# An encoder layer on one core: the second 512 tokens' rows into the opening's buffers, longer leads, gate tiles three ahead, and residual rows as whole tiles

## The chip, the cores and the metric

The kernel runs on one core of a Trainium2 chip. The core has five engines with instruction streams of their own: TensorE (PE, matmuls and transposes by matmul), VectorE (DVE), ScalarE (ACT), GpSimd (POOL) and SyncE (SP), which issues nearly all transfers in this kernel; sixteen DMA engines carry them out. The metric is device time in microseconds; smaller is better.

## The reference

Two sequences, one of 1024 tokens (the prompt, s = 0) and one of 2048 (the sample, s = 1), with 1024 channels, go through one layer of a bidirectional encoder. Sixteen learned meta tokens stand in front of each.

```python
xn = _rmsnorm(h, g_pre)
proj = xn @ w_in + b_in                                  # 6672 columns
na_q, na_k, na_v, na_z, ml_qk, ml_v, ml_z, ml_o, ml_g, mg = jnp.split(proj, SPLIT_IDX, axis=-1)
ya = _neighbourhood_attention(na_q, na_k, na_v, na_rpb)  # 8 heads of 64, windows of 8 x 16 on a grid 64 wide
ya = (ya * jax.nn.silu(na_z)) @ w_a
yb = (_mlstm_branch(ml_qk, ml_v, ml_g, ml_o, ml_conv_w, ml_head_g) * jax.nn.silu(ml_z)) @ w_b   # 4 heads of 128, both directions
ga, gb = jnp.split(jax.nn.sigmoid(mg), 2, axis=-1)
y = (ga * ya + gb * yb) @ w_out
return h + _rmsnorm(y, g_post)
```

All is float32.

## The kernel before

**Matmuls.** A float32 product is made of three matmuls on split operands (`mm3`, lines 155 to 157): high by high, high by low, low by high. Every weight and every activation is therefore split into a rounded high part (ACT) and a remainder (DVE). Weights come in units of 512 KB: `wload` loads a raw unit into a `wraw` tile, `wpump` (L250, L251) splits it into `whi` and `wlo`, and both parts are also stored, so that later uses load the parts (L243) and no raw unit. Before the opening ends raw units lie in a pool of its own (`xp`, four buffers); after it in the main pool `wp` (two buffers).

**Two streams of work.** `dense` is a generator for the projections and the output: it goes through `PLAN`, a list of column groups (m: mLSTM columns, n: attention columns, g: gate columns) for stretches of 1024 tokens, and then six output blocks of 512 tokens ("f", two of the prompt and four of the sample). `sparse` is a generator for the mixers in the order mLSTM of the prompt, attention of the prompt, mLSTM of the sample, attention of the sample. `run` (L1617) weaves them: each step of `sparse` yields a number of microseconds, and `dense` is advanced until its own yields have used that number up. The numbers are constants at L118: `A_NA` for a step of attention, `A_A` for a step of the mLSTM outputs, `A_D` for a step of the mLSTM states, `A_G` for one of its gates; a dense step of 512 columns counts 0.235 for each matmul and one of 256 columns 0.12. Each attention unit (a head and a quarter of the columns of eight grid rows) takes four steps: scores, scaling, transposition, output. The order of PE's instructions is the order in which these generators write them. The order on the other engines and on SP's queue is made by a planner, which simulates the program and takes what is ready, in the order of writing where several are. Each engine then runs in that order, and an instruction that waits holds up those behind it.

**Opening.** The first 512 tokens' activations come transposed (`xt`, four loads) and in rows (`tokens`, four loads of 512 KB into tiles `xr`). `xsplit` scales and splits the transposed ones. The rows serve the RMS norm: `rsum` squares and sums them on ACT (tile `xsq`, L287) and takes the inverse root by Newton steps on DVE (L141 to L146), `rdiag` (L299, L301) writes it into diagonals, and `rrows` (L307) lets PE broadcast it. The projections of these tokens are evacuated with that factor, so they wait for the broadcast in their third or fourth column; its place in PE's order is fixed in `group`. Nine buffers named `xr` in `xp` hold the opening's tiles of both kinds and the meta tokens. The second 512 tokens' transposed tiles are loaded in the opening into four `xr` buffers of `wp`; their rows are loaded later, in `build_half` (L394), into these same four buffers, one behind each `xsplit`. The pool `xp` is closed at the end of the opening.

**Attention.** `na` (L733) prepares the first head in six steps of `na_prep`: loads first, then splits. Between the loads and the first split lie `14 - 8 * s` steps of `A_NA`, that is 14 for the prompt and 6 for the sample.

**mLSTM states.** `ml_states` (L1089) runs once for each of four heads. It loads two blocks, yields `A_D`, begins the convolution (`cv`), yields, ends it (`kf`, L1112), yields, and then transposes `kf` on PE (L1148) in a loop. For the first head the loads go into memory that the gates' tiles free.

**Output blocks.** `final` (L1429) makes a block of 512 tokens. For each of eight column tiles `ft` it multiplies the two branches by their weights (branch 1, then 0), and DVE multiplies each product by a gate tile `tg` (L1465) loaded from DRAM. `gates(ft + 2)` is called at the end of step `ft`. Gate tiles of both branches share four buffers under the tag `stT`. The sum is split (`mh` L1468, `mlo` L1469) and multiplied by `w_out` (L1495 to L1497). Beside that second half runs `yload` for the next block, whose `yr` tiles have four buffers under the tag `st`. The norm and the residual of a block are a generator, `final_out` (L1545), advanced twice in each `ft` of the next block: it loads half rows of the input (128 x 512, `xres`, three ahead) into `st` buffers too, and DVE adds them (L1568). The last block has a list of its own, `self.last`, whose tiles lie in `st` and `wraw` buffers.

Of the kernel before, what the change touches and what calls it, by code (L numbers as in the profile page):

```python
# [9 lines left out]
F32 = mybir.dt.float32  # L10
# [3 lines left out]
ALU = mybir.AluOpType  # L14
# [3 lines left out]
P = 128  # L18
TCARGS = dict(schedule_with_timeline_sim=True)
D = 1024  # L20
# [15 lines left out]
WU = 264  # L36
# [78 lines left out]

NBW = 4
C512, C256 = 0.235, 0.12
A_NA, A_D, A_A, A_G = 1.12, 1.63, 1.84, 1.3  # L118


class K:
# [218 lines left out]
    def opening(self, xp):  # L340

        nc, wp, cp = self.nc, self.wp, self.cp
# [11 lines left out]
        toks = self.tokens(0, 0, (0, 1), xp, 9)  # L354
# [3 lines left out]
        self.xnext = [self.xtload(0, 512, e, wp, 4) for e in (0, 1)]  # L358
        self.wload(4)
        self.xnext += [self.xtload(0, 512, e, wp, 4) for e in (2, 3)]  # L360
        x = self.xparts()
        self.xs.append(tuple(x))
        g = self.gpre.rearrange("p (k a) -> p k a", a=1).to_broadcast([P, KT, NM])
# [16 lines left out]
        dg, dm = self.rdiag(res[0], dt), dt[:NM, 512:]  # L380
# [13 lines left out]
    def build_half(self, s, t0, res):  # L394

        nc, wp = self.nc, self.wp
        if (s, t0) in self.xkept:
            yield
            yield "scaled"
            x = []  # L400
# [7 lines left out]
        if s == 0:  # L408
# [7 lines left out]
            if not self.done:  # L416
# [1 line left out]
                nc.tensor.matmul(p[:, :KT], self.ident, g, start=True, stop=True)  # L418
                g = self.cp.tile([P, KT], F32, name="gx")
                nc.vector.tensor_copy(g, p[:, :KT])  # L420
            x, toks, r = self.xparts(), [], []
            for e in range(4):
                self.xsplit(x, xts[e], e, 0, g)
                if not self.done:
                    toks += self.tokens(s, t0, (e,), wp, 4)
                    self.wflush(2)
                yield
            res.append(tuple(x))
            if self.done:
                return  # L430
            self.wflush()
            yield
            yield from self.rsum(toks, r)
            nc.vector.tensor_copy(self.rc[:, 4:8], r[0])
            dg = self.rdiag(r[0], toks[0][0])
            self.rwait[s, t0] = lambda: self.rrows(dg, self.rr[:, 1], "sm")
        else:
            toks, r = self.tokens(s, t0, range(4), wp, 4), []
            yield
# [14 lines left out]
            x = self.xparts()  # L454
# [278 lines left out]
    def na(self, s, rts):  # L733
# [3 lines left out]
        with tc.tile_pool(name=f"na{s}{rts[0]}", bufs=1, side="right", reuse_waits="tile") as np_:  # L737
# [10 lines left out]
            prep = self.na_prep(np_, s, rows, heads, 0)  # L748
            for k in range(6):
                next(prep, None)  # L750
                for _ in range(2 if k else 14 - 8 * s):
                    yield A_NA
            self.na_bias(rows, heads, 0)
            cur, nxt = self.head, None
# [334 lines left out]
    def ml_states(self, mp, s, h, g, NB, sts):  # L1089
# [42 lines left out]

        load(0)
        load(1)
        yield A_D
        conv_a(0)
        yield A_D
        conv_b(0)
# [290 lines left out]
    def final(self, s, b, nxt):  # L1429
# [10 lines left out]
        def gates(ft):  # L1440
            if ft < KT:
                tgs[ft] = []
                for br in (1, 0):
                    tg = fp.tile([P, n], F32, name="tg", tag="stT", bufs=4)
                    nc.sync.dma_start(tg, self.GT[s][8 * br + ft][:, t0:t0 + n])
                    tgs[ft].insert(0, tg)

        gates(0)
        gates(1)
        for ft in range(KT):  # L1450
            w = self.wtake(1)[0]
            ms = tgs.pop(ft)
            for br in (1, 0):
                for k in range(4 * br, 4 * br + 4):
                    while k not in self.yk:
                        if next(self.ygen) == "wait":
                            yield True
                p = self.psum("pj", [P, 512])
                for k in range(4 * br, 4 * br + 4):
                    self.mm3(p, w[0][:, k, :], w[1][:, k, :], yh[:, k], yl[:, k], start=k % 4 == 0, stop=k % 4 == 3)  # L1460
                    if k % 4 == 1:
                        yield 6 * C512
                if not br:
                    self.wdone()
                nc.vector.scalar_tensor_tensor(ms[br], ms[br], 1.0, p, op0=ALU.add, op1=ALU.mult)  # L1465
                if not br:
                    nc.vector.tensor_tensor(ms[0], ms[0], ms[1], op=ALU.add)
                    nc.scalar.activation(mh[:, ft], ms[0], AF.Copy)  # L1468
# [76 lines left out]
    def final_out(self, s, t0, yt, ssq, a, b):  # L1545

        nc, fp, i = self.nc, self.wp, self.i
        src, out = (i["x_prompt"], self.o[0]) if s == 0 else (i["x_sample"], self.o[1])
        todo = [(tt, slice(t0 + tt * P, t0 + tt * P + P), c) for tt in range(a, b) for c in (slice(0, 512), slice(512, D))]
        xr = [self.last.pop(0) for _ in todo] if self.last else []  # L1550
# [12 lines left out]
        nc.vector.tensor_scalar(sv[:, a:b], sv[:, a:b], 1.0 / D, 16.0 * EPS, op0=ALU.mult, op1=ALU.add)  # L1563
        r = self.rsqrt8(fp, sv[:, a:b], [P, b - a])
        yield
        for j, (tt, rows, c) in enumerate(todo):
            y = yt[tt][:, c]
            nc.vector.scalar_tensor_tensor(y, y, r[:, tt - a:tt - a + 1], xr[j], op0=ALU.mult, op1=ALU.add)  # L1568
            nc.sync.dma_start(out[rows, c], y)
            load(j + 3)  # L1570
            yield


    def dense(self, ctx):
# [4 lines left out]
        with tc.tile_pool(name="xp", bufs=1, side="right", reuse_waits="tile") as xp:  # L1579
            self.wrp = xp, 4  # L1580
            self.opening(xp)
        self.y = self.fout = None
        meta, post = True, None
        for j, (s, t0, cols) in enumerate(PLAN):
# [108 lines left out]
```

## Time and profile before

| what | value |
|---|---|
| median of 3 runs | 2869.04 us (2866.74 to 2869.99) |
| the profiled execution | 2862.5 us |
| its span, first to last instruction | 2860.7 us |
| mean granted TensorE clock in it | 0.993 |
| PE busy | 2798.8 us |
| DVE busy | 1799.6 us |
| ACT busy | 1307.1 us |
| moved by DMA | 661.43 MB, mean 231 GB/s |

How to read the lines that follow. A row of waits names the engine and line that waited, what released it, the sum of the waits, their number and the longest. A row of a stretch gives its bounds, its length, the busy time of PE, PE's weight loads, DVE, ACT and POOL, each with the number of instructions, then the granted clock (1.00 is full), the share in which the DMA engines were busy, and GB/s. A row of the timeline gives the start, the length, the engine, the line, the operation, its output and inputs, and in brackets how long the engine had stood idle and what released it. A row of the chain of work gives the start, the length and the step; that chain is followed backwards from the last instruction.

### The profile page before, as it was taken

The numbers are of one execution on the slowest core, as the hardware profiler recorded it, in microseconds if no ns is written. First come the engines' busy times: TensorE is split into PE (matmuls) and PEld (weight loads), VectorE is DVE, ScalarE is ACT, GpSimd is POOL, SyncE is SP. The second block draws the span as 40 slices with busy tenths as digits, with TensorE's granted clock in tenths as the row PEclk, the third lists the DMA queues.
The fourth block names the chain that finished last, engine by engine and source line by source line (L and its number), as shares of the span: only waits on it lengthen the run. The fifth ranks groups of instructions, "written<-read, shape, count | busy, mean of one in ns | idle before, by whom it ended". The sixth has DMA issues, their size and how long they took to land.

```text
span 2860.7 us, 49242 instructions
## 1 busy us (share of the span) xinstructions
PE 2798.8 (98%) x17312; PEld 2489.1 (87%) x17312; DVE 1799.6 (63%) x4931; ACT 1307.1 (46%) x3135; POOL 16.1 (1%) x103
## 2 busy tenths in 40 slices
PE   8999999999999999999999999999999999999998
PEld 7998898999799988888988888888887988889887
DVE  4232688576466654556667666574678787787844
ACT  5112556444444443355455555453455554545421
POOL 0000000000000000000000000000000000000000
PEclk9999999999999999999999999999999999999999
DMA  9455768755876654675656786656679898998875
GB/s 370 162 187 194 236 211 296 275 182 177 312 236 188 179 166 133 187 278 164 206 194 207 245 283 188 192 185 192 202 243 337 278 326 271 293 291 252 291 261 179
DMA packets 385001, 661.43 MB, mean 231 GB/s; under 512 B 51984, under 2 KB 200928, under 8 KB 384752
## 3 DMA queue, kind: packets, MB, share of 16 engines
q1 hardware_dynamic: 383632, 655.58, 69.5%
q0 software_dynamic: 1120, 2.69, 0.4%
q8 instruction: 137, 2.24, 0.3%
q14 instruction: 112, 0.92, 0.1%
HBM read 455.90 MB, written 202.22 MB: 230 GB/s over the span
## 4 chain that ended last, share of the span: by engine, by line
PE 81%; DMA 10%; DVE 5%; ACT 1%; issue 1%; SPq 1%; DVEq 0%; ACTq 0%
PE pj L155 14%; PE pj L156 13%; PE pj L157 13%; PE pj L575 6%; PE pj L576 6%; PE pj L577 6%; PE pj L1497 3%; PE pj L1495 3%; PE pj L1496 3%; PE sm L884 3%; PE tr L872 2%; DMA tg<-gt 2%; PE sm L157 1%; PE sm L156 1%; PE sc L848 1%
## 5 line engine op out<-in xcount | busy, mean ns | idle before, releaser
L155 PE MATMUL pj<-xh,whi 128*128 128x512 f32 (+1 forms) x1792 | 706.2, 394 | 2.4 <-ACT whi L250 1.8
L156 PE MATMUL pj<-xl,whi 128*128 128x512 f32 (+1 forms) x1792 | 690.4, 385 | 0.1
L157 PE MATMUL pj<-xh,wlo 128*128 128x512 f32 (+1 forms) x1792 | 688.8, 384 | 0.3 <-DVE wlo L251 0.3
L575 PE MATMUL pj<-whi,xh 128*128 128x256 f32 (+3 forms) x1576 | 451.0, 286 | 0.0
L576 PE MATMUL pj<-wlo,xh 128*128 128x256 f32 (+3 forms) x1576 | 444.6, 282 | 0.0
L577 PE MATMUL pj<-whi,xl 128*128 128x256 f32 (+3 forms) x1576 | 444.4, 282 | 0.0
L157 PEld LDWEIGHTS pj<-xh,wlo 128*128 128x128 f32 x1792 | 337.9, 189 | 72.1 <-DVE wlo L251 0.5
L155 PEld LDWEIGHTS pj<-xh,whi 128*128 128x128 f32 x1792 | 338.3, 189 | 62.2 <-ACT whi L250 2.6
L156 PEld LDWEIGHTS pj<-xl,whi 128*128 128x128 f32 x1792 | 338.5, 189 | 56.8 <-issue 1.0
L575 PEld LDWEIGHTS pj<-whi,xh 128*128 128x128 f32 (+1 forms) x1576 | 294.4, 187 | 1.6 <-ACT st L505 0.3
L576 PEld LDWEIGHTS pj<-wlo,xh 128*128 128x128 f32 (+1 forms) x1576 | 294.1, 187 | 1.0
L577 PEld LDWEIGHTS pj<-whi,xl 128*128 128x128 f32 (+1 forms) x1576 | 294.0, 187 | 0.9
L1495 PE MATMUL pj<-whi,mh 128*128 128x256 f32 x768 | 220.7, 287 | 5.1 <-ACT mh L1468 2.6
L855 ACT ACTIVATE prb<-sc,mx 128x384 f32<-128x384 f32 (+2 forms) x192 | 120.0, 625 | 223.2 <-DVE mx L851 216.9
L1497 PE MATMUL pj<-whi,mlo 128*128 128x256 f32 x768 | 217.5, 283 | 2.3 <-DVE mlo L1469 2.3
L1496 PE MATMUL pj<-wlo,mh 128*128 128x256 f32 x768 | 217.2, 283 | 0.0
L875 DVE TENSOR_TENSOR pts<-tr,pts 96x512 fp32r<-96x512 f32 (+2 forms) x192 | 131.5, 685 | 84.3 <-ACT pts L874 83.0
L155 PE MATMUL pj<-yh,whi 128*128 128x512 f32 x384 | 156.6, 408 | 5.9 <-DVE tg L1465 5.9
L874 ACT ACTIVATE pts<-tr 96x512 fp32r<-96x512 f32 (+2 forms) x192 | 114.0, 594 | 103.2 <-PE tr L872 102.5
L1495 PEld LDWEIGHTS pj<-whi,mh 128*128 128x128 f32 x768 | 146.2, 190 | 7.5 <-ACT mh L1468 3.1
L156 PE MATMUL pj<-yl,whi 128*128 128x512 f32 x384 | 152.0, 396 | 0.0
L157 PE MATMUL pj<-yh,wlo 128*128 128x512 f32 x384 | 152.0, 396 | 0.0
(271 smaller groups left out, 5043.8 us busy)
## 6 DMA issues: line engine op xcount, KB each, us to landing
whi<-wh SPq DMA_DIRECT2D x176, 512.0 KB
wlo<-wl SPq DMA_DIRECT2D x176, 512.0 KB
wraw<-wu SPq DMA_DIRECT2D x64, 512.0 KB
wh<-whi SPq DMA_DIRECT2D x64, 512.0 KB
wl<-wlo SPq DMA_DIRECT2D x64, 512.0 KB
gt<-st SPq DMA_DIRECT2D x96, 256.0 KB
tg<-gt SPq DMA_DIRECT2D x96, 256.0 KB
xt<-xt SPq DMA_DIRECT2D x32, 512.0 KB
```

Of the source, the lines that this page charges most:

```text
L155: mm(out, ah, bh, start=start, stop=False)
L156: mm(out, ah, bl, start=False, stop=False)
L157: mm(out, al, bh, start=False, stop=stop)
L575: nc.tensor.matmul(o, xh, wh, start=k == 0, stop=False)
L576: nc.tensor.matmul(o, xh, wl, start=False, stop=False)
L577: nc.tensor.matmul(o, xl, wh, start=False, stop=k == KT - 1)
L855: nc.scalar.activation(pr_[:, :N].rearrange("p (b a c) -> p b a c", b=4, c=8), sc[:, :N].rearrange("p (a b c) -> p b a c", b=4, c=8), AF.E ...
L874: nc.scalar.activation(pts[:ks, :, 0, :], pt[:ks], AF.Copy)
L875: nc.vector.tensor_tensor(pts[:ks, :, 1, :], pt[:ks], pts[:ks, :, 0, :].bitcast(F32), op=ALU.subtract)
L1495: nc.tensor.matmul(o, mh[:, k, xs], wh, start=k == 0, stop=False)
L1496: nc.tensor.matmul(o, mh[:, k, xs], wl, start=False, stop=False)
L1497: nc.tensor.matmul(o, ml[:, k, xs], wh, start=False, stop=k == KT - 1)
```

## The change

Seven edits are made.

1. The rows of the second 512 tokens are loaded at the end of the opening's loads, as four more tiles `xr` in `xp`, where nine buffers now serve thirteen tiles; `build_half` loads none and no longer writes out all remaining weight parts in a step of its own. `xp` stays open until the broadcast of these tokens has been written.
2. The step costs `A_NA` and `A_A` go from 1.12 to 1.1 and from 1.84 to 1.82.
3. The lead of the first attention head goes from 14 to 17 steps for the prompt and stays at 6 for the sample.
4. The first head of each mLSTM yields 6.0 us more between its loads and its convolution.
5. Gate tiles are asked for three steps ahead instead of two. Those of branch 1 stay under the tag `stT`, those of branch 0 go under `st`, with four buffers each.
6. `final_out` loads whole rows (128 x 1024) into the two `wraw` buffers of `wp`, two ahead, and asks for the next one after the second half of a tile has been used.
7. The last block still takes its residual tiles from `self.last`.

```diff
-A_NA, A_D, A_A, A_G = 1.12, 1.63, 1.84, 1.3
+A_NA, A_D, A_A, A_G = 1.1, 1.63, 1.82, 1.3
...
         self.xnext += [self.xtload(0, 512, e, wp, 4) for e in (2, 3)]
+        self.toks = self.tokens(0, 512, range(4), xp, 9)
         x = self.xparts()
...
-            x, toks, r = self.xparts(), [], []
+            x, r = self.xparts(), []
             for e in range(4):
                 self.xsplit(x, xts[e], e, 0, g)
                 if not self.done:
-                    toks += self.tokens(s, t0, (e,), wp, 4)
                     self.wflush(2)
                 yield
             res.append(tuple(x))
             if self.done:
                 return
-            self.wflush()
-            yield
-            yield from self.rsum(toks, r)
+            yield from self.rsum(self.toks, r)
             nc.vector.tensor_copy(self.rc[:, 4:8], r[0])
-            dg = self.rdiag(r[0], toks[0][0])
-            self.rwait[s, t0] = lambda: self.rrows(dg, self.rr[:, 1], "sm")
+            dg = self.rdiag(r[0], self.toks[0][0])
+
+            def rows():
+                self.rrows(dg, self.rr[:, 1], "sm")
+                self.xp.close()
+            self.rwait[s, t0] = rows
...
-                for _ in range(2 if k else 14 - 8 * s):
+                for _ in range(2 if k else 17 - 11 * s):
                     yield A_NA
...
         load(1)
-        yield A_D
+        yield A_D + (0.0 if h else 6.0)
         conv_a(0)
...
-                    tg = fp.tile([P, n], F32, name="tg", tag="stT", bufs=4)
+                    tg = fp.tile([P, n], F32, name="tg", tag=("st", "stT")[br], bufs=4)
...
-        gates(0)
-        gates(1)
+        for ft in range(3):
+            gates(ft)
...
-                    gates(ft + 2)
+                    gates(ft + 3)
...
-        def load(j):
-            if len(xr) <= j < len(todo):
-                x = fp.tile([P, 512], F32, name="xres", tag="st", bufs=4)
-                nc.sync.dma_start(x, src[todo[j][1], todo[j][2]])
-                xr.append(x)
-
-        for j in range(3):
-            load(j)
+        def load(tt):
+            if tt < b:
+                xr.append(fp.tile([P, 4 * WU], F32, name="xres", tag="wraw", bufs=2)[:, :D])
+                nc.sync.dma_start(xr[-1], src[t0 + tt * P:t0 + tt * P + P, :])
+
+        if not self.last:
+            load(a)
+            load(a + 1)
         yield
...
-        for j, (tt, rows, c) in enumerate(todo):
-            y = yt[tt][:, c]
-            nc.vector.scalar_tensor_tensor(y, y, r[:, tt - a:tt - a + 1], xr[j], op0=ALU.mult, op1=ALU.add)
-            nc.sync.dma_start(out[rows, c], y)
-            load(j + 3)
-            yield
+        for tt in range(a, b):
+            x = None if self.last else xr.popleft()
+            for c in (slice(0, 512), slice(512, D)):
+                y = yt[tt][:, c]
+                nc.vector.scalar_tensor_tensor(y, y, r[:, tt - a:tt - a + 1], self.last.pop(0) if self.last else x[:, c], op0=ALU.mult, op1=ALU.add)
+                nc.sync.dma_start(out[t0 + tt * P:t0 + tt * P + P, c], y)
+                if c.start:
+                    load(tt + 2)
+                yield
```

More of the change, by code (lines that the diff above doesn't have):

```diff
@@ L1548, in final_out @@
         src, out = (i["x_prompt"], self.o[0]) if s == 0 else (i["x_sample"], self.o[1])
-        todo = [(tt, slice(t0 + tt * P, t0 + tt * P + P), c) for tt in range(a, b) for c in (slice(0, 512), slice(512, D))]
-        xr = [self.last.pop(0) for _ in todo] if self.last else []
-        def load(j):
-            if len(xr) <= j < len(todo):
-                x = fp.tile([P, 512], F32, name="xres", tag="st", bufs=4)
-                nc.sync.dma_start(x, src[todo[j][1], todo[j][2]])
-                xr.append(x)
-        for j in range(3):
-            load(j)
+        xr = deque()
+        def load(tt):
[5 more added lines that the diff above has]
+            load(a + 1)
         yield
@@ L1578, in dense @@
         self.requests()
-        with tc.tile_pool(name="xp", bufs=1, side="right", reuse_waits="tile") as xp:
-            self.wrp = xp, 4
-            self.opening(xp)
+        self.xp = ExitStack()
+        xp = self.xp.enter_context(tc.tile_pool(name="xp", bufs=1, side="right", reuse_waits="tile"))
+        self.wrp = xp, 4
+        self.opening(xp)
         self.y = self.fout = None
```

## The prediction

> **What bounds the kernel now.** I read the page first, then the busy time by stages, then who made TensorE wait, then the granted clock right behind each wait, and last the chain of work around the places that the diff touches.
>
> ```profile
> span 2860.7 us, 49242 instructions
> ...
> PE 2798.8 (98%) x17312; PEld 2489.1 (87%) x17312; DVE 1799.6 (63%) x4931; ACT 1307.1 (46%) x3135; POOL 16.1 (1%) x103
> ...
> PE 81%; DMA 10%; DVE 5%; ACT 1%; issue 1%; SPq 1%; DVEq 0%; ACTq 0%
> ```
>
> TensorE (PE) is the bound: it idles 2860.7 - 2798.8 = 61.9 us. The change removes and adds no matmul, so it can win no more than this and what a lowered clock costs. Where the 61.9 us lie (the first number of a row's body is its length, the second PE's busy time):
>
> ```profile
> 0.00:100.00 100.00, 91.67 (x591) 81.16 (x592) 41.61 (x101) 43.20 (x74) 1.20 (x18) 0.97 0.86 320
> ...
> 300.00:350.00 50.00, 47.70 (x308) 43.56 (x307) 31.19 (x84) 26.78 (x70) 2.56 (x14) 0.97 0.68 218
> ...
> 750.00:800.00 50.00, 46.28 (x208) 37.22 (x207) 25.03 (x48) 20.67 (x37) 0.00 (x0) 0.97 0.97 348
> 800.00:1150.00 350.00, 350.00 (x2337) 322.09 (x2336) 204.69 (x524) 151.11 (x335) 1.74 (x16) 1.00 0.57 174
> 1150.00:1200.00 50.00, 43.54 (x349) 42.36 (x348) 21.83 (x81) 16.29 (x48) 0.00 (x0) 0.93 0.61 172
> ...
> 2100.00:2740.00 640.00, 614.20 (x3902) 551.06 (x3902) 514.42 (x1201) 325.70 (x769) 2.04 (x4) 0.99 0.89 288
> 2740.00:2861.00 121.00, 108.06 (x721) 98.53 (x719) 54.36 (x142) 16.93 (x56) 0.00 (x0) 0.99 0.64 231
> ```
>
> So 8.3 us in the opening, 2.3 where the first mLSTM starts, 3.7 where the first attention starts, 6.5 where the second mLSTM starts, 25.8 while the output blocks run beside the second attention, 12.9 in the last block and the tail. Who held PE:
>
> ```profile
> PE tr L872 <- DVE prb L864: 12.9, 9, 3.7
> PE pj L155 <- DVE tg L1465: 5.9, 5, 2.3
> PE tr L1148 <- DVE kf L1112: 5.4, 1, 5.4
> PE sm L307 <- ACT xr L299: 4.5, 1, 4.5
> ...
> PE sc L847 <- DVE stk L825: 3.2, 1, 3.2
> PE pj L1495 <- ACT mh L1468: 2.6, 1, 2.6
> ```
>
> Three waits occur once each (L1148, L307, L847 behind stk), and the diff has an edit for each of the three. The first two rows, 12.9 and 5.9 us, belong to the output blocks. A wait is also paid a second time. Right after each longer one the granted clock (the third number from the end) is halved:
>
> ```profile
> 60.30:65.30 5.00, 5.00 (x11) 3.30 (x12) 2.29 (x4) 2.19 (x4) 0.00 (x0) 0.50 1.02 410
> 314.50:317.80 3.30, 3.30 (x17) 3.30 (x17) 1.80 (x7) 1.50 (x7) 0.33 (x2) 0.50 1.06 395
> 771.90:775.20 3.30, 3.30 (x10) 2.52 (x9) 2.34 (x6) 1.78 (x4) 0.00 (x0) 0.50 1.05 404
> 1191.60:1195.00 3.40, 3.40 (x17) 3.40 (x18) 2.16 (x5) 2.42 (x7) 0.00 (x0) 0.50 0.60 168
> 2174.80:2178.00 3.20, 3.20 (x11) 2.61 (x10) 2.86 (x7) 1.65 (x2) 0.00 (x0) 0.50 1.02 308
> 2211.00:2215.60 4.60, 4.60 (x24) 4.60 (x23) 3.19 (x7) 3.02 (x8) 0.00 (x0) 0.50 0.70 255
> ...
> 2662.90:2666.20 3.30, 3.30 (x12) 2.72 (x11) 3.27 (x7) 0.67 (x2) 0.00 (x0) 0.50 1.05 404
> ```
>
> PE is busy throughout these stretches at half speed, so each costs half its length: 2.5, 1.65, 1.65, 1.7, 1.6, 2.3 and 1.65 us.
>
> **Opening: rows of the second 512 tokens.** Before, their four loads are issued inside build_half, after each xsplit; the squares, the Newton steps and the diagonal follow, and PE's row broadcast (L307) waits for them.
>
> ```profile
> 46.37 0.59 SPq L330 DMA_DIRECT2D xr<-x_prompt  x1
> ```
>
> ```profile
> 51.33 1.09 ACT L250 ACTIVATE whi<-wraw 128x1056 fp32r<-128x1056 f32 x1 [4.48 <-DMA mq<-st]
> 52.32 1.04 ACT L287 ACTIVATE xsq<-xr 128x1024 bf16<-128x1024 f32 x1
> ```
>
> The last of the four is issued at 46.37, the first square starts at 52.32, and ACT had stood idle 4.48 us in front of it. After the change the loads go into buffers whose readers are the first xsplits and squares, so by my estimate they are issued some 20 us sooner. Four squares (4 x 1.04 us) then fit into ACT's idle time ahead of 51.33, and the chain behind them is done 5 us or more sooner, against a wait of 4.5. What covers it: PE has matmuls of the second half until the broadcast. Gain 4.5 + 2.5 = 7.0 us. Low end 4.5, if a smaller wait still halves the clock. High end of cost: the 2 MB enter a DMA system that is 0.86 busy in this stage, at 320 GB/s 6.6 us of transfer, and whatever is queued behind them on SP moves by up to that: stores of weight parts and, before, these same rows. The next raw weights are not needed before the second job, so I charge nothing, and 2 us in the range. Keeping the opening's pool open until the broadcast delays only loads that go into its memory later, the first mLSTM's constants, which that stage (300 to 350) does not need so early.
>
> **First attention: 14 steps of lead become 17.** The lead is 17 x 1.10 - 14 x 1.12 = 3.0 us of dense work more before PE's first score.
>
> ```profile
> 771.48 0.44 PE L848 MATMUL sc<-kx,qB 128*128 128x384 f32 x1 [0.47 <-DVE kx L829]
> ```
>
> ```profile
> 756.39 9.48 DMA xt<-xt
> ```
>
> The wait is 3.2 + 0.47 = 3.7 us: the head's splits stand behind the next half's, which wait for an xt load of 9.48 us. 3.0 of it goes and 0.7 stays. Whether the clock still drops with that is open; I take half of 1.65. Gain 3.0 + 0.8 = 3.8, ends 1.5 and 5.4. Late next is kx, the 0.47.
>
> **mLSTM: 6 us more before the first convolution, in both.** In the second one the load is issued at 1179.25, when the gates' buffers come free, and lands 5.93 us later; on DVE kf then stands behind a decay tile whose load ends at 1190.67.
>
> ```profile
> 1179.25 5.93 DMA raw<-mk
> ...
> 1187.04 3.63 DMA um<-ud
> ```
>
> PE comes 6.0 us later to a wait of 5.4: it goes, with 0.6 to spare. Gain 5.4 + 1.7 = 7.1; low end 3, because the decay load may move along. In the first mLSTM the 2.3 us come later, in its second step, where ACT is crowded; the lead moves PE and ACT alike. I take nothing (ends -4.0 and +1.5).
>
> The Trainium skill (TensorE: Matmul & The Clock Gate, What's actually happening) says that the clock falls back to half after an idle window of about 3.4 us. By that rule the 0.7 us left at the attention's start cost no clock, and its term would be 3.0 + 1.65 = 4.65. The trace sides with it only in part: waits of 2.3 us in all (300 to 350) were followed by a halved clock.
>
> **Step costs 1.12 to 1.10 and 1.84 to 1.82.** From the loops: attention takes 264 + 520 steps, the mLSTM outputs 136 + 232. 784 x 0.02 + 368 x 0.02 = 23.0 us less dense work is laid beside the sparse work, 12.0 + 3.3 more in the leads. About 8 us of matmuls move behind the last attention unit. That is PE work at the same price, so 0. The side effect is density: a unit has 4 x 0.02 = 0.08 us less cover. From 800 to 1150, most of it beside the first attention, PE is busy 350.00 of 350 us at 1.12, so I price it at 0 there; it speaks only beside the output blocks.
>
> **Output blocks: gates three ahead, residual rows elsewhere.** DVE works in order; while it waits for a load there, the scaling of attention (prb) stands behind it.
>
> ```profile
> DVE tg L1465 <- DMA tg<-gt: 26.4, 15, 4.3
> ...
> DVE yo L1568 <- DMA xres<-x_sample: 8.5, 4, 3.3
> DVE yo L1568 <- DMA xres<-x_prompt: 3.2, 3, 1.9
> ```
>
> ```profile
> 2174.44 0.83 PE L872 MATMUL tr<-ident,prb 128*128 128x128 f32 x4 [2.07 <-DVE prb L864]
> 2302.26 0.63 PE L872 MATMUL tr<-ident,prb 128*128 128x128 f32 x4 [1.77 <-DVE prb L864]
> 2418.23 0.63 PE L872 MATMUL tr<-ident,prb 128*128 128x128 f32 x4 [1.95 <-DVE prb L864]
> 2662.68 0.94 PE L872 MATMUL tr<-ident,prb 128*104 128x128 f32 x4 [1.96 <-DVE prb L864]
> ```
>
> ```profile
> 2279.27 6.08 DMA xres<-x_prompt
> ...
> 2418.28 8.10 DMA tg<-gt
> ...
> 2646.82 6.58 DMA xres<-x_sample
> ```
>
> One ft step is 24 matmuls, 5.6 us at the code's own 0.235, plus the attention's share; a third step of lead exceeds the longest gate wait of 4.3. Gates no longer share four buffers between both branches, and residual rows no longer compete with the yr loads for st. The transfers grow from 256 to 512 KB, in half the number, with the lead of three half rows kept. Best case: all 5.9 us of tg, these four prb waits (7.75), and the clock behind two of them (1.6 + 1.65) go: 16.9 us. Worst: nothing, because DMA is 0.89 busy over this stage and an earlier load makes another one later. I take half, 8.5. The other waits (heads' loads, L1495 behind mh, the last weights) I leave as they are; they will fall in other places, which I hold for +-6 us. The last block's residual tiles now wait for the last gates, with half a block of time.
>
> **Sum.** 7.0 + 3.8 + 7.1 + 8.5 = 26.4 us; less 1.4 for small new waits in the crowded stages: 25. The profiled execution took 2862.5 us (span 2860.7), 6.5 below the median 2869.0 of the runs shown. Its like after the change is 2837.5, and the median forecast 2869 - 25 = 2844. About 0.2%, 5.7 us, is what a measurement of this kernel can tell from no change.
>
> **Rivals.** First: the output blocks are bound by transfers, and earlier loads gain nothing there. For it: share 0.89 at 288 GB/s over 640 us. Against: the last 121 us are at 0.64 and still have a gate wait, and the opening moved 410 GB/s. Then 17.9 us remain: 2851. Chance 0.20. The Trainium skill (DMA: Bandwidth & Descriptors, Specifications) gives about 358 GB/s of HBM per core, a limit by which such stretches are full; the 410 GB/s here pass it.
>
> Second: the leads only move the wait, to kx and to the decay tile, and the output blocks gain nothing either. Opening 7.0, attention 1.5, mLSTM 3: gain 11.5, 2857.5. For it: 0.47 behind kx and the um row. Chance 0.10.
>
> Third, slower: the third gate pair (512 KB) and larger residual tiles (1 MB against 768 KB at a block's start) put 0.75 MB in front of the heads' loads in SP's one queue, 2.6 us at 288 GB/s. ACT and DVE then stand at a head's split more often. Its price from the trace: the mh wait of 2.6 us, followed by 2.3 of halved clock, 4.9. Twenty-four heads, about five per block, run in this stage. At one more such wait in each of five blocks it is 24.5 us: 2869 - 17.9 + 24.5 = 2875.6. It decides from four (19.6 against 17.9). For it: DVE is 514.4 of 640 busy. Against: these loads do land somewhere today, in the same blocks. Chance 0.08.
>
> Fourth: the edit in the opening does nothing, because SP still issues the rows late or ACT orders the squares late: 19.4 without its 7.0 and with small waits counted, 18 us, 2851. Chance 0.05.
>
> **Chances and range.** The forecast has 0.57, with its own range 2834 to 2854. From 2829 (16.9 in the output blocks and 4.0 in the first mLSTM) to 2863 all but the slower case and a poor second rival are held. Faster by over 0.2%: 0.57 + 0.20 + 0.05 + 0.05 (half of the second, with its spread) = 0.87, which I lower to 0.85; the same 0.06; slower 0.09.
>
> **What would show it.** Right: no wait at L307 and L1148, at most 1 us at L847 behind stk or kx; no 0.50 clock after them; the xsq squares of the second rows before 50 us; DVE's waits for tg under 10 us. Wrong: PE's busy time unchanged but its idle time in the output blocks above 35 us; ACT or DVE waiting longer for kr, qr or whi; new waits of PE in the first 50 us for weights.

## The result and the profile after

| | before | after |
|---|---|---|
| median of 7 runs | 2867.28 us (2864.1 to 2870.18) | 2849.97 us (2837.03 to 2858.18) |
| the profiled execution | 2862.5 us | 2845.39 us |
| its span | 2860.7 us | 2843.6 us |

The ratio of the times is 0.9933, with an interval of 0.9913 to 0.9954, which is 19 us less. On another occasion, beside the kernel before on the same chip, the changed kernel gave 0.9906 (0.9889 to 0.9923), 27 us less. Both profiled executions lie 4.6 to 4.8 us below their medians, so their spans can be compared as they stand. The head of the page of the changed kernel:

```profile
span 2843.6 us, 49257 instructions
...
PE 2795.7 (98%) x17312; PEld 2488.8 (88%) x17312; DVE 1796.3 (63%) x4931; ACT 1306.4 (46%) x3135; POOL 16.1 (1%) x103
```

PE's idle time fell from 61.9 to 2843.6 - 2795.7 = 47.9 us, which is 14.0; its busy time fell by 3.1 with the same matmuls. Together 17.1, the difference of the spans. Each trace is of one execution: the seven of the changed kernel spread over 21 us, and a second trace of it (the last run below) idles 23.8 us in the output blocks where this one idles 20.7, so differences of a few microseconds between the stages of two traces are not told from this spread. The stages of the changed kernel, in the columns of the prediction's table of stretches:

```profile
0.00:100.00 100.00, 96.16 (x641) 85.58 (x642) 42.64 (x103) 43.46 (x75) 1.20 (x18) 1.00 0.87 325
300.00:350.00 50.00, 49.53 (x329) 45.25 (x328) 32.78 (x84) 26.21 (x68) 2.62 (x14) 1.00 0.70 248
750.00:800.00 50.00, 46.34 (x229) 39.58 (x228) 22.75 (x46) 18.93 (x36) 0.00 (x0) 0.93 0.99 325
1150.00:1200.00 50.00, 47.10 (x378) 45.11 (x377) 25.03 (x91) 18.45 (x56) 0.00 (x0) 1.00 0.52 156
1200.00:2100.00 900.00, 894.76 (x4682) 756.65 (x4680) 560.88 (x1743) 459.26 (x1165) 4.08 (x22) 1.00 0.65 209
2100.00:2740.00 640.00, 619.31 (x3989) 559.44 (x3988) 515.45 (x1202) 325.06 (x777) 2.04 (x4) 0.99 0.90 292
2740.00:2861.00 121.00, 93.12 (x597) 84.25 (x596) 49.59 (x131) 13.16 (x44) 0.00 (x0) 0.97 0.56 200
```

The fifth stage of the kernel before, which the prediction did not show:

```profile
1200.00:2100.00 900.00, 897.70 (x4741) 761.24 (x4740) 563.44 (x1745) 458.81 (x1167) 4.08 (x22) 1.00 0.64 209
```

Idle time of PE by stage, before and after (the last stage ends at 2843.6): opening 8.3 to 3.8, first mLSTM 2.3 to 0.5, first attention 3.7 to 3.7, start of the second mLSTM 6.5 to 2.9, its continuation 2.3 to 5.2, output blocks 25.8 to 20.7, last block and tail 12.6 to 10.5 (the prediction's 12.9 counts up to 2861; the span ends at 2860.7). Who held PE in the changed kernel (line numbers below the edits are two or three higher):

```profile
PE tr L874 <- DVE prb L866: 12.3, 7, 3.3
PE sc L849 <- ACT prb L857: 5.9, 4, 3.0
PE pj L577 <- DMA whi<-wh: 2.9, 1, 2.9
PE sc L155 <- ACT qh L1228: 2.6, 1, 2.6
...
PE tr L1150 <- DVE kf L1114: 1.2, 1, 1.2
```

The broadcast's wait (4.5), the gates' (5.9) and the wait behind stk (3.2) have no row left, and kf went from 5.4 to 1.2. New are the weight loads and qh. The transposition behind prb still costs what it did, 12.3 against 12.9, and the score behind ACT's prb costs 5.9 against 4.5. Three places in the changed kernel's timeline, first on PE, then on SP and ACT in the opening, then on ACT at 1877:

```profile
790.67 0.49 PE L577 MATMUL pj<-whi,xh 128*128 128x264 f32 x1 [2.88 <-DMA whi<-wh]
791.94 0.59 PE L578 MATMUL pj<-wlo,xh 128*128 128x264 f32 x1 [0.79 <-DMA wlo<-wl]
1882.54 0.33 PE L155 MATMUL sc<-qh,kh 128*128 128x128 f32 x1 [2.63 <-ACT qh L1228]
```

```profile
20.33 2.86 SPq L330 DMA_DIRECT2D xr<-x_prompt  x4
```

```profile
30.28 1.07 ACT L287 ACTIVATE xsq<-xr 128x1024 bf16<-128x1024 f32 x1
...
40.51 1.04 ACT L287 ACTIVATE xsq<-xr 128x1024 bf16<-128x1024 f32 x1
```

```profile
1877.18 5.00 ACT L321 ACTIVATE xh<-xt,gpre 128x512 fp32r<-128x512 f32 x8
```

In the opening the last row load was issued at 46.37 before; now the four leave from 20.33 on and the squares fall between 30 and 42 us. At 1877 eight splits of a next half, 5.00 us on ACT, stand in front of the split qh that the second mLSTM needs; that is where the shifted streams meet. Behind both places on PE, the weights and qh, the clock is halved, in these stretches:

```profile
790.90:795.00 4.10, 3.31 (x15) 3.06 (x15) 0.24 (x1) 0.00 (x0) 0.00 (x0) 0.50 1.05 307
1885.00:1889.50 4.50, 4.50 (x17) 3.92 (x17) 3.52 (x13) 2.49 (x7) 0.00 (x0) 0.50 1.01 366
```

Last, the output blocks from DVE's and ACT's side, from 2100 us on, before and then after:

```profile
ACT yh L1403 <- DMA yr<-ya: 17.4, 12, 4.8
ACT yh L1403 <- DMA yr<-yb: 1.4, 1, 1.4
...
DVE yl L1404 <- ACT yh L1403: 10.7, 8, 5.0
```

```profile
DVE yl L1406 <- ACT yh L1405: 20.8, 14, 3.7
...
ACT yh L1405 <- DMA yr<-yb: 21.9, 11, 3.9
ACT yh L1405 <- DMA yr<-ya: 13.4, 10, 2.6
```

DVE's 26.4 us of waits for gates have no row any more. ACT's waits for the branches' rows (yr), which now share the buffers `st` with the gates of branch 0, rose from 18.8 to 35.3 us, and DVE's for yh behind them from 10.7 to 20.8.

### The profile page after: what moved, and what is told of

It reads as the page before. It is cut to its first block, busy times and chain, and to the rows that moved or that the text cites. A ratio compares the mean times of both kernels' runs of the same rounds, so it can differ in the third digit from the quotient of the medians.

```text
span 2843.6 us, 49257 instructions
## 1 busy us (share of the span) xinstructions
PE 2795.7 (98%) x17312; PEld 2488.8 (88%) x17312; DVE 1796.3 (63%) x4931; ACT 1306.4 (46%) x3135; POOL 16.1 (1%) x103
## 4 chain that ended last, share of the span: by engine, by line
PE 85%; DMA 8%; DVE 5%; ACT 1%; issue 1%; SPq 0%; DVEq 0%; ACTq 0%
PE pj L155 15%; PE pj L156 14%; PE pj L157 14%; PE pj L577 6%; PE pj L578 6%; PE pj L579 6%; PE pj L1499 3%; PE pj L1497 3%; PE pj L1498 3%; PE sm L886 3%; PE tr L874 2%; DMA wlo<-wl 1%; DMA um<-ud 1%; PE sm L157 1%; PE sc L849 1%; PE sm L156 1%
```

## The experiments

The table holds every run; each ratio stands against the kernel before on the same chip, and the microseconds are the ratio applied to that kernel's median. A ratio is not the quotient of the two medians and can differ from it, most for the first row (6.4 us by the medians). The traced executions of the mLSTM lead, of gates and residual rows, and of the gates with the attention lead are the slowest of their kernels, so their traces show less of a gain than the table.

| kernel | median, us | before, us | ratio (interval) | gain, us |
|---|---|---|---|---|
| opening edit alone | 2861.16 | 2867.51 | 0.9992 (0.998 to 1.0005) | 2.3 |
| mLSTM lead alone | 2864.51 | 2867.51 | 0.9985 (0.9975 to 0.9996) | 4.3 |
| attention lead alone | 2875.77 | 2867.51 | 1.0031 (1.0017 to 1.0044) | -8.9 |
| gates and residual rows | 2851.07 | 2867.51 | 0.9942 (0.9927 to 0.9958) | 16.6 |
| step costs alone | 2858.19 | 2866.91 | 0.9971 (0.9958 to 0.9985) | 8.3 |
| gates alone | 2850.3 | 2866.91 | 0.9943 (0.9923 to 0.9964) | 16.3 |
| residual rows alone | 2865.4 | 2866.91 | 0.9996 (0.998 to 1.0011) | 1.1 |
| the change with the old step costs | 2846.95 | 2866.91 | 0.993 (0.9909 to 0.9951) | 20.1 |
| gates, opening, mLSTM lead | 2836.06 | 2867.2 | 0.9896 (0.9877 to 0.9915) | 29.8 |
| gates, attention lead | 2837.27 | 2867.2 | 0.9898 (0.988 to 0.9916) | 29.2 |
| the change with a lead of 14 | 2838.64 | 2867.2 | 0.9898 (0.988 to 0.9916) | 29.2 |
| the change once more | 2844.75 | 2870.09 | 0.9906 (0.9889 to 0.9923) | 27.0 |

**The opening alone.** The main line of the edit; the rest is as in the whole diff.

```diff
+        self.toks = self.tokens(0, 512, range(4), xp, 9)   # in the opening; build_half loads none
```

> The kernel before with the opening's edit alone (rows of the second 512 tokens loaded into the opening's buffers). Theory A, the waits add up: PE's 4.5 us behind the diagonal (L307) and the halved clock after it (2.5 us) go, about 1.5 us come back behind an evacuation, the rest of the trace keeps its idle time within 3 us: 5 to 7 us faster. Rival B, any edit re-deals the order on DVE, ACT and SP and with it the waits of all later stages: the opening gains the same, but the idle time after 300 us changes by 5 us or more either way and the time is anywhere from 15 faster to 5 slower.

The edit does in its place what it was priced for: the stage's busy time goes from 91.67 to 96.68 of 100 us. By the ratio it gains 2.3 us, and the interval includes none; by the medians it gains 6.4. Seven of its twelve executions lie at 2858 to 2861 us and five at 2866 to 2872, so how much of the start's saving arrives at the end stays open. In the trace the idle time behind 300 us rises by 1.7 us only, within the 3 us of theory A. In the output blocks, which the edit does not touch, the idle time is 27.8 us (25.8 before), and a wait for prb of 6.46 us is there, longer than any of the kernel before. Two views, stretches and PE's timeline:

```profile
0.00:100.00 100.00, 96.68 (x640) 85.58 (x641) 42.55 (x103) 43.48 (x75) 1.20 (x18) 1.00 0.87 325
...
2100.00:2740.00 640.00, 612.22 (x3898) 550.16 (x3897) 512.90 (x1194) 324.31 (x766) 2.04 (x4) 0.98 0.89 286
```

```profile
2535.84 1.09 PE L874 MATMUL tr<-ident,prb 128*128 128x128 f32 x4 [6.46 <-DVE prb L866]
```

**The mLSTM lead alone.**

```diff
-        yield A_D
+        yield A_D + (0.0 if h else 6.0)
```

> The kernel before with 6 us more between loads and first convolution of both mLSTMs alone. Theory A: the wait of 5.4 us at the second mLSTM's start falls to 0 to 1.5, its clock loss of 1.7 goes, and in the first mLSTM the 2.3 us (and 1.65 of clock) that the prediction left standing go too, as in the changed kernel's trace: 8 to 10 us faster. By the prediction's own term (first mLSTM unchanged): 7.1 faster. Rival B: the shift of 6 and 12 us between dense and sparse work re-deals the later waits: idle time in the output blocks (25.8 us from 2100 to 2740) changes by 5 us or more.

The gain of 4.3 us is less than the 8 to 10 of theory A and the 7.1 of the prediction, and the idle time of the blocks, 26.2 us, did not move as rival B has it. The wait at L1148 is gone, and so is the one at the first attention (PE is busy for all of the 50 us from 750 to 800), which this edit was not made for. Their place on PE's timeline is taken by these two, one soon after and one at the start of the last block, whose rows of the attention are not yet there:

```profile
1208.91 0.58 PE L157 MATMUL sm<-vwh,ktl 128*128 128x260 f32 x1 [3.37 <-DVE ktl L1152]
...
2765.92 0.80 PE L155 MATMUL pj<-yh,whi 128*128 128x512 f32 x1 [6.62 <-ACT yh L1403]
```

**The attention lead alone.**

```diff
-                for _ in range(2 if k else 14 - 8 * s):
+                for _ in range(2 if k else 17 - 11 * s):
```

> The kernel before with 17 instead of 14 steps of lead for the first attention alone. The prediction's term: 3.8 us faster, at most 0.7 us of wait left at the first score. The theory from the changed kernel's trace: the wait goes from the first score to the weight loads of the next unit a few us later (2.9 and 0.8 us behind whi and wlo, with a halved clock of up to 3.4 us of cost): between 1 us faster and 2 us slower, PE idle from 750 to 810 still 3 us or more.

It is slower by 8.9 us. The stk wait at the start is gone, and as the theory had it the next weights are waited for instead (1.60 and 0.89 us at 801). The idle time that the edit adds appears 1300 us later. PE's waits, DVE's from 2080 us on, and the stretch of the output blocks:

```profile
PE pj L155 <- DVE tg L1465: 15.5, 8, 3.9
```

```profile
DVE tg L1465 <- DMA tg<-gt: 41.8, 23, 3.8
```

```profile
2100.00:2740.00 640.00, 603.61 (x3769) 537.12 (x3768) 506.62 (x1176) 318.80 (x749) 2.04 (x4) 0.98 0.90 286
```

PE idles 36.4 us in the blocks against 25.8. DVE waits for gates 41.8 against 26.4, and PE for DVE's gate product 15.5 against 5.9. No instruction of the blocks was edited; only the point of the attention at which a gate is asked for differs by three steps. The rest of what this trace loses is in PE's busy time, 2807.9 us against 2798.8 with the same matmuls, at a mean granted clock of 0.991 against 0.993.

**Gates and residual rows together, and each alone.** The first kernel has the edits 5 and 6 of the change, the second this diff alone, the third edit 6 alone, of which the second diff shows the main lines.

```diff
-                    tg = fp.tile([P, n], F32, name="tg", tag="stT", bufs=4)
+                    tg = fp.tile([P, n], F32, name="tg", tag=("st", "stT")[br], bufs=4)
...
-        gates(0)
-        gates(1)
+        for ft in range(3):
+            gates(ft)
...
-                    gates(ft + 2)
+                    gates(ft + 3)
```

> The kernel before with the output blocks' two edits alone (gate tiles three ahead under two tags, residual rows as whole tiles in the raw weights' buffers). The prediction's term: 8.5 us faster, up to 16.9. The theory from the changed kernel's trace: DVE's waits for gate loads (26.4 us) go below 6 and those for residual rows (11.7) to 5, but branch 0's gates hold st buffers, so ACT waits for yr loads 30 us or more instead of 18.8, PE's waits behind the scaled scores stay at 11 to 13 us, and the gain is what PE waited directly for gates, 5 to 8 us. Rival: transfers are the bound there and nothing is gained (within 3 us).

> The kernel before with the gate tiles alone (three ahead, branch 0 under st); residual half rows stay in st too. If the gates carry the blocks' gain of 16.6 us: 10 us faster or more, DVE's waits for gate loads below 6 us instead of 26.4. If st becomes too narrow with gates, yr and residual rows in four buffers: DVE's waits for residual rows above 15 us instead of 11.7 and ACT's for yr above 25 instead of 18.8, and the gain is 5 us or less.

```diff
-                x = fp.tile([P, 512], F32, name="xres", tag="st", bufs=4)
+                xr.append(fp.tile([P, 4 * WU], F32, name="xres", tag="wraw", bufs=2)[:, :D])
```

> The kernel before with the residual rows alone (whole tiles in the raw weights' buffers); gates stay two ahead under stT. If the two edits add: 3 to 7 us faster, DVE's waits for residual rows 8 us or less instead of 11.7, for gates 20 or more as before. If the residual edit only makes room in st for the gates and is worth nothing alone: within 3 us.

The gates carry it: 16.3 us alone, 16.6 with the residual rows (5 to 8 was expected), and the residual rows alone 1.1 with an interval on both sides of none. DVE's waits from 2100 us on, PE's, and the stretch, with the gates alone:

```profile
DVE yo L1568 <- DMA xres<-x_sample: 23.2, 13, 3.7
DVE yo L1568 <- DMA xres<-x_prompt: 10.4, 7, 3.1
DVE tg L1465 <- DMA tg<-gt: 1.5, 1, 1.5
```

```profile
PE sc L847 <- ACT prb L855: 11.9, 12, 1.8
PE tr L872 <- DVE prb L864: 6.4, 6, 2.0
```

```profile
2100.00:2740.00 640.00, 620.13 (x3994) 556.84 (x3993) 515.60 (x1211) 327.61 (x779) 2.04 (x4) 1.00 0.91 292
```

The wait for gates falls from 26.4 to 1.5 us, while that for residual rows, which still compete for `st`, rises from 11.7 to 33.6. That hardly holds PE: it idles 19.9 us against 25.8, and the stretch's mean clock is 1.00 against 0.99. So a late residual row is cheap here and a late gate is not; the edit that shortens the first (to 4.6 us in the whole change) buys nothing that these runs can tell.

Where the 16.3 us come from is less clear than that they come. Of the 12.1 us between the two traced executions, 6.8 are idle time of PE and 5.3 busy time, at a mean clock of 0.996 against 0.993. PE's waits for the gate product fall from 5.9 to 0.9 us and those for mh and mlo behind it from 4.9 to 0.6. The two prb rows hold 18.3 us together against 17.4. With gates and residual rows together the gain is the same, yet its trace, of a slow execution, idles 26.5 us in the blocks:

```profile
2100.00:2740.00 640.00, 613.49 (x3937) 552.29 (x3936) 515.28 (x1205) 327.35 (x773) 2.04 (x4) 0.99 0.89 289
```

The edit also gives the gate tiles eight buffers, four of them shared with the yr tiles, in place of four; whether the third step or the buffers bring the gain was not tried.

**Step costs alone, and the change without them.**

```diff
-A_NA, A_D, A_A, A_G = 1.12, 1.63, 1.84, 1.3
+A_NA, A_D, A_A, A_G = 1.1, 1.63, 1.82, 1.3
```

> The kernel before with the two step costs alone (1.12 to 1.10, 1.84 to 1.82). The prediction's term: 0. Theory C, the cut is a balance: about 23 us less dense work beside the sparse work, so the last attention unit ends some 20 us earlier; the kernel before has little wait there to lose, so 0 to 4 us faster, with no new wait in the attention's units from 830 to 1150. Rival, density: less cover for each unit, PE's waits behind the scaled scores rise from 12.9 us to 18 or more and it is 3 to 10 us slower. If the parts add, what is left for this edit of the whole gain of 19 is 5 us.

> The changed kernel with the step costs of before (1.12 and 1.84). The prediction's term for them: 0, so the ratio stays at 0.993. Theory C: with the leads of 12 and 3.3 us the attention of the sample ends later, and the last block waits for its rows as in the run with the mLSTM lead alone (6.6 us there, with halved clock behind it): the last attention unit ends about 23 us later than in the changed kernel, PE waits 4 us or more for the last block's yh, and it is 6 to 12 us slower than the changed kernel, ratio 0.995 to 0.997.

Alone, the lower costs gain 8.3 us, more than either theory has. In that trace PE idles 20.8 us in the blocks, as little as in the whole change, although gates are two ahead and DVE waits 23.6 us for them; a shift of the streams alone can do that. The whole change without the lower costs is at 0.993 (0.995 to 0.997 was expected) against 0.9933 and 0.9906 with them, so in the whole they are worth nothing that these runs can tell. That is so although the wait at the start of the last block, which the lower costs were held to avoid, is there without them:

```profile
2750.67 0.79 PE L155 MATMUL pj<-yh,whi 128*128 128x512 f32 x1 [5.75 <-ACT yh L1405]
```

**Gates with the starts.** By now the single edits had given 2.3, 4.3, -8.9, 8.3, 16.3 and 1.1 us, 23.4 in sum, against 19.2 and later 27.0 for the whole. That they agree is chance if the starts' gains are lost where late gates re-deal the waits. Then a start edit must do better on top of gates three ahead. The two kernels combine the diffs shown above: gates with opening and mLSTM lead, and gates with the attention lead.

> The kernel before with three edits: gate tiles, opening, mLSTM lead; old costs, old attention lead, residual half rows in st. Theory D: the starts' gains (7.0 and 7.1 by the prediction) are real, but alone they were given back in the output blocks, where two-ahead gates make every shift costly; with gates three ahead they add: 0.9943 becomes 0.989 to 0.991, and PE's idle time from 2100 to 2740 stays at 20 us or less, as in the run with the gates alone. Rival E: each shift re-deals the waits whatever the gates do; then the start is bought back again and the ratio is 0.993 to 0.996.

> The kernel before with two edits: gate tiles and the attention's lead of 17. Alone the lead cost 9 us, with DVE's gate waits up from 26.4 to 41.8 us and PE's own from 5.9 to 15.5. Theory D: with gates three ahead that loss is gone, and the lead is worth its own small gain or nothing: ratio 0.992 to 0.995, DVE's gate waits below 5 us. Rival F: the loss sits at the attention's start (weights late behind the heads' loads): then it stays, ratio 0.996 or more.

The lead that alone costs 8.9 us costs nothing here: with it the gates gain 29.2 us, more than the 14 to 23 us of theory D, and without it 16.3. These 12.9 us were measured on two chips on two occasions, and all three kernels of the later one came out between 0.9896 and 0.9898, so a gain by the lead is not shown. That its loss is gone is shown: the sum of the two single results would be 7.4; the gap of 21.8 us is far beyond the intervals and beyond the 7.8 us by which the whole change differed between two occasions. DVE's waits from 2080 us on and the stretch of that kernel:

```profile
DVE yo L1568 <- DMA xres<-x_sample: 17.7, 13, 5.0
...
DVE tg L1465 <- DMA tg<-gt: 4.8, 3, 1.8
```

```profile
2100.00:2740.00 640.00, 624.62 (x4040) 562.66 (x4039) 517.00 (x1217) 328.87 (x784) 2.05 (x4) 0.99 0.90 293
```

PE idles 15.4 us in the blocks where the same lead alone left 36.4, and DVE waits for gates 4.8 us instead of 41.8. The other combination gains 29.8, as theory D has it, against a sum of 22.9; this gap of 6.9 is no larger than the 7.8 between occasions, so it points the same way and does not prove it. Its page and its waits of PE:

```profile
PE 2783.9 (98%) x17312; PEld 2479.9 (88%) x17312; DVE 1797.8 (64%) x4931; ACT 1307.3 (46%) x3135; POOL 16.2 (1%) x103
```

```profile
PE pj L155 <- ACT yh L1405: 12.4, 1, 12.4
PE tr L874 <- DVE prb L866: 6.9, 8, 2.0
```

PE's busy time is 14.9 us below that of the kernel before, with the same matmuls, and its idle time, 2828.5 - 2783.9 = 44.6 us, 17.3 below. The largest wait is a single one: 12.4 us for the attention's rows at the last block, which ends at 2728.95 and so is most of the 20.7 us of idle time in the blocks. (This profiled execution, 2830.23 us, is the fastest of its kernel.) So the combination wins nearly half of its time by the clock: laid over PE's instructions, the clock record has PE at work under a halved clock for 31.2 us in the kernel before and 7.1 here, which is worth 12.1 us. The changed kernel, with 28.4 us of such work and 2795.7 busy, does not.

**The change with a lead of 14, and the change once more.**

```diff
-                for _ in range(2 if k else 17 - 11 * s):
+                for _ in range(2 if k else 14 - 8 * s):
```

> The changed kernel with the attention's lead back at 14 steps. If the lead gives nothing because its wait moves to the weights (2.9 and 0.8 us at 790 in the changed kernel's trace, with 6.8 us of halved clock): the first score waits 2 to 4 us again and the weights do not, and the ratio stays within 0.0015 of 0.9933. If the lead's 3.8 us are real: 0.9945 to 0.995. If the lead costs: 0.992 or less.

> The changed kernel as it is, once more, beside its own runs of the kernel before. Two kernels that differ from it by the attention's lead, or by fewer edits, came out at 0.9898, it at 0.9933, on other occasions. If that difference of 10 us is the lead's wait behind the weights: ratio 0.992 to 0.995 again, and again 2.5 us or more of waits behind whi and wlo near 790. If it is the spread between occasions: 0.989 to 0.991.

With 14 steps PE waits once at the start, 1.63 us for the first score, and no weight is missing there. Its 0.9898 looked better than the change's 0.9933, but the change itself came to 0.9906 when it was run again, although its trace waits for the same two weights as before (2.15 and 0.88 us). Whether the longer lead is worth anything in the whole change stays open. So does whether the two combinations above, 0.9896 and 0.9898, beat it: all three were measured together, on one chip, and the change on other occasions. All three beat the kernel before clearly.

## Why the prediction was right, and where its terms were not

Direction and size came out: 25 us were forecast and 17.3 (by the medians), 19.2 (by the ratio) and 27.0 (on the second occasion) measured; the median 2850.0 lies inside the forecast's own range of 2834 to 2854. It is right as a sum, less so by its terms, and that the sum fits is in part luck. The three starts' edits, 17.9 us by the prediction, measured -2.3 one by one; the blocks, 8.5, and the step costs, 0, measured 16.6 and 8.3. On top of the gates the opening and the mLSTM lead add 13.5 us, against 14.1 by the prediction, but across two occasions.

- **Opening, 7.0.** Right in its place: the squares are done by 42 us, no wait and no halved clock are left at L307, and 8.3 us of idle time became 3.8. Alone the edit gave 2.3 by the ratio and 6.4 by the medians. That what is saved at a start arrives at the end was taken for granted; these runs do not settle it.
- **First attention, 3.8.** Wrong in its place. The stk wait went, but "late next is kx" named the wrong successor: it is the next weights (2.88 and 0.79 us), and the halved clock with them, the row of 750 to 800 at 0.93. The stage's idle time stayed at 3.7. The later run of the change shows the same two waits, the change with the old step costs and the combination with the opening and the mLSTM lead show none, so they hang on a few us of phase.
- **mLSTM, 7.1.** Mis-sized. kf waits 1.2 us and no longer at half clock, which is 4.2 + 1.7 = 5.9; then 2.6 us and a halved clock return behind qh. Alone it gave 4.3. The first mLSTM, taken at nothing, won 1.8 within its ends.
- **Step costs, 0.** Not told from 0 in the whole change; alone they gained 8.3, which the density argument did not foresee.
- **Output blocks, 8.5.** Mis-sized: the half should have been the whole. Gates three ahead alone gave 16.3, next to the best case of 16.9. But they did not do it as written: of the prb waits, 12.3 of 12.9 us stayed in the changed kernel, and with the gates alone the two prb rows did not fall in sum. That the longer waits for yr and yh, whose buffers the gates took, keep the prb waits up fits the rows and was not tested. The share of the residual rows is nothing that can be told from 0.
- **Small new waits, 1.4.** Too little: weights at 790, qh at 1882, 6.3 us together, with a halved clock behind both.
- **The range.** Its low end of 2829 does not come out of the terms named for it: 2844 - (16.9 - 8.5) - 4.0 is 2831.6.

**Rivals.** That the blocks are bound by transfers fell: at a DMA share of 0.91 against 0.89, and 292 GB/s against 288, the gates' edit alone gained 16.3. That the leads only move the wait is true of the attention's start; the mLSTM lead gained 4.3 us with the gates two ahead. As a forecast of the whole it fell, because the gates' edit gains. That heads' loads are delayed and the kernel gets slower fell: ACT's waits for kr and qr went from 12.4 to 7.7 us. The loads that were delayed are yr, 16.5 us more of ACT's waits. That the opening's edit does nothing fell in its place, though alone it can't be told from nothing in the time.

**The clock behind a wait.** The prediction left open whether a short wait halves the clock, and wrote that each longer one is followed by a halved clock. The second does not hold in the kernel before: behind waits of 2.29, 2.20 and 2.20 us (at 2438.40, 2709.00 and 2789.71) the clock stayed full, behind 1.96 and 2.07 us it was halved. The Trainium skill (TensorE: Matmul & The Clock Gate, What's actually happening) has the clock fall after about 3.4 us of idling; the changed kernel does not agree: after waits of 1.81 us (mh, at 2444.27) and 0.82 us (mlo, at 2445.59) the next stretch is at half clock. The last section works out what decides.

```profile
2444.27 0.39 PE L1497 MATMUL pj<-whi,mh 128*128 128x256 f32 x1 [1.81 <-ACT mh L1470]
...
2445.59 0.39 PE L1499 MATMUL pj<-whi,mlo 128*128 128x256 f32 x1 [0.82 <-DVE mlo L1471]
```

What stays open besides: why the whole change differed by 7.8 us between two occasions, with intervals that overlap; and how much a buffer of its own for branch 0's gates would win by leaving `st` to the yr tiles, which was not tried.

## What to carry to other kernels

Price a late load by more than the wait of the bounding engine that carries its name: the gates cost PE 5.9 us by name and were worth 16.3, and in the trace the rest is the waits behind the same gate product and the clock. Where several edits each save a wait at a start, first remove the place further on where each shift makes other loads late; an edit tried alone ahead of that can come out far from its worth, as the lead did with -8.9 alone and no loss on top of the gates. When a buffer is lent to a load, look at once who else lived in it: the residual rows could spare `st`, while the yr tiles were waited for longer, 35.3 us against 18.8.

## What the runs showed of the hardware

The price of a wait is not its length. In the changed kernel's output blocks PE waited 1.71, 1.80, 1.81, 2.43, 2.79, 2.96 and 3.32 us at seven places; behind the first two the clock stayed full, at the other five it was granted at 0.50 for 3.41 us, the record of the clock says. That is up to 1.7 us on top of each wait.

What decides is not the single wait either. The halved stretches of this trace start at 790.81, 1883.07, 2166.38, 2446.27, 2528.19, 2572.57, 2647.66 and 2838.81 us; all distances between them are whole multiples of 3.413 us (2528.19 - 2446.27 is 24 of them), and each stretch lasts one or two. So cut the trace into slots on this grid: PE idled 1.98 us or more in the eight slots ahead of the halved stretches, and at most 1.71 in every other slot at full clock. The wait of 1.80 us falls across two slots (PE idles 1.14 us in all in the first); the one of 1.81 lies for the most part in one slot with the 0.82 behind mlo, and PE idles 2.22 us in it. The slots with these two and with the 1.71, and the one that follows 2446.27:

```profile
2282.36:2285.77 3.41, 1.70 (x11) 1.17 (x10) 3.29 (x10) 1.05 (x3) 0.00 (x0) 1.00 1.04 412
2319.90:2323.32 3.42, 2.36 (x20) 2.15 (x19) 1.49 (x4) 1.68 (x5) 0.00 (x0) 1.00 1.03 392
2442.86:2446.27 3.41, 1.19 (x7) 0.98 (x8) 3.02 (x8) 3.39 (x7) 0.00 (x0) 1.00 1.11 265
2446.27:2449.69 3.42, 3.42 (x19) 3.42 (x18) 3.32 (x9) 1.74 (x7) 0.00 (x0) 0.50 1.08 282
```

In all fourteen traces, up to PE's last matmul, no slot at full clock with more than 1.9 us of idle time was followed by a full clock, and only one with less than 1.6 (1.40) by a halved one; between 1.6 and 1.9 both occur. A halved clock thus follows about half a slot of idling, in one wait or several.

At the other end stands the 12.4 us wait of the combined kernel: the clock was granted at 0.50 mostly while PE stood still, and only some 3.7 us of work ran under it (2728.95 to 2732.64; the second row shows 3.40 of them).

```profile
2719.20:2728.90 9.70, 0.00 (x0) 0.00 (x0) 1.50 (x2) 0.63 (x1) 0.00 (x0) 0.50 0.45 150
2729.00:2732.40 3.40, 3.40 (x8) 2.38 (x8) 2.00 (x3) 0.02 (x1) 0.00 (x0) 0.50 0.45 92
```

So 12.4 us of waiting in one piece cost about 12.4 + 1.8 us, where the seven waits above, 16.8 us in all, were followed by five halved stretches. The other surprise is how far a small shift reaches: three steps, 3.4 us by the code's count, more work ahead of one head went with 10.6 us more of PE's idle time in stages 1300 us later, where two traces of the changed kernel differ by 3.1.
